# One more item in a layer's first group of matmuls, its split weights held in another pool

## The chip, the cores and the metric

The kernel runs on one NeuronCore of a Trainium2 chip. The metric is device time in microseconds (us) of one execution, the median over runs. The time before is 2758.85 us, the median of 3 runs (2755.78 to 2760.88).

## What is computed

The reference is one inference step of a two-layer trunk on 128 context tokens and 512 latent tokens (640 together), model width 1024. Each layer runs three mixers on one normalised input and then a feed-forward block. Cut to what the change touches:

```python
h = rms_norm(x, lp['g_pre1']) * (1 + sc1) + sh1
(cb, cc, cx, aq, ak, av, dn_q, dn_k, dn_v, dn_z, dn_beta, dn_a, gate_logits) = jnp.split(
    h @ lp['w_in'], SPLIT_IDX, axis=-1)
ya = (cb * depthwise_conv(cc * cx, lp['conv_w'])) @ lp['w_pa']
...
# gated DeltaNet, 4 heads of 128
qkv = jax.nn.silu(depthwise_conv(jnp.concatenate([q_raw, k_raw, v_raw], axis=-1), conv_w))
g = -jnp.exp(a_log) * jax.nn.softplus(a_logit + dt_bias)
...
o = rms_norm(o, norm_g) * jax.nn.silu(z)
```

The change is about `z = dn_z`, a 1024 by 512 slice of the input projection, 128 columns for each head. Its value is needed only at the end, when the head's output `o` is gated.

## The kernel before

**A linear layer.** Activations lie as 8 tiles of 128 channels by 640 tokens, each split into a high and a low part (`hh`, `hl`). A weight block is 128 x 4 x 128: it is loaded into `wraw` (L361 or L376, 256 KB, three buffers, issued by SyncE's queue SP), ScalarE (ACT) casts it to `whi` (L94), VectorE (DVE) forms `wlo` (L95), and TensorE (PE) runs three matmuls for each of 4 channel tiles (L365 to L367) on 320 tokens, which is half of them. So one output of 128 columns takes two blocks, and 24 matmuls for each half of the tokens. `whi` and `wlo` have four buffers each (`NW = 4`); a PSUM tile `l` has three (`NL = 3`), so the fourth `l` in a row waits until the first has been copied out.

**The group.** A layer begins with `group(items)`: it loads and splits the weights of all items, runs the first half of the tokens through all of them and then the second half, so the first half can run while the second half of `hh`, `hl` is still being made. Items with a pool name (`"C"`, `"E"`) hold their split weights there through both halves (`wkh`, `wkl`, or `wk` in `"E"`). The items are k, q, v of DeltaNet head 0, the gate logits (`lin`, L825, raw weights), and z of head 0. In layer 1 the previous layer's residual norm runs as `side`, one step after each item.

**What follows.** `gz()` is `dn_gates_tail`: matmuls `bgG` (L836, L850, L860) with a chain of small ACT and DVE steps in between (`bn`, `gb`), ending in `rws` (L862), which is written to memory (`gd`, L863) and read back four times, spread over partitions, as `rowb` (L917, three buffers). From `rowb` come `egl` (L972), `Dt` (L967, L977) and the rest of the DeltaNet preparation. Meanwhile `dn_post` runs k, q and v through a convolution (`dy`, L579 to L581, DVE), a sigmoid (`ds`, ACT) and a product (`dz`, DVE); `nat` (L911) transposes `dz` of k and v, and `kk` (L958) multiplies. The other linear layers are woven between these as filler (`fillc`), by costs that the generators yield: first z of the second head (`dn_z(l, 1)`), then the convolution branch (`cc`, whose first output is copied by L449 into `ccs`), while k, q, v of head 1 follow as `padc` (L873 copies). The Tile framework keeps each engine's instructions in the order in which it scheduled them, so on every engine an instruction that waits holds back all behind it.

Of the kernel before, what the change touches and what calls it, by code (L numbers as in the profile page):

```python
# [52 lines left out]
def tile_trunk(ctx: ExitStack, tc: tile.TileContext, I: dict, O: list, layers=DEPTH):  # L53
# [7 lines left out]
    def slot(name, shape=(P, NT), dt=F32, tag="F"):  # L61
        n = {"H": NH_, "C": NC_, "F": NF_}[tag]
        return sb.tile(list(shape), dt, tag=tag, name=name, bufs=n)
# [33 lines left out]
    def drain(g):  # L97
        for _ in g or ():
            pass
# [296 lines left out]
    def linear(src, acts, ev):  # L396


        pb = {}
        i0 = 0  # L400
        for hi, lo, nk in wblocks(src, len(acts)):
            for h in range(2):
                if i0 == 0:
                    pb[h] = lbank()[:, :HF]
                for j in range(nk):
                    ah, al = acts[i0 + j]
                    mm3(pb[h], hi[:, j, :], lo[:, j, :], hv(ah, h), hv(al, h), i0 + j == 0, i0 + j == len(acts) - 1)
                if i0 + nk == len(acts):
                    ev(h, pb[h])
            i0 += nk  # L410

    def group(items, side=None):


        bl = [b if callable(b) or isinstance(b, list) else wblocks(b, len(a), k) for b, a, _, k in items]
        for h in range(2):
            for b, (_, a, ev, _) in zip(bl, items):
                if callable(b):
                    b(h)
                else:  # L420
                    lin_half(b, a, h, ev)
                if h == 0:
                    next(side or iter(()), None)
            drain(side)

    def sig_ev(dst, keep=None, halves=False):

        def ev(h, pb):
            A.activation(hv(dst, h), pb, AF.Exp, scale=-1.0)  # L429
            if keep is not None:  # L430
                V.tensor_copy(hv(keep, h), pb)
            if halves:
                sig_tail(hv(dst, h))
            elif h:
                sig_tail(dst)
        return ev
# [24 lines left out]
    def store_x(src):  # L461
        for k in range(KD):
            SY.dma_start(out=xd[k], in_=src[k])
# [341 lines left out]
    def dn_gates(l):  # L805

        raw = slot("wg", (P, KD, 32), tag="C")
        G.memset(raw, 0.0)
        c0 = COL["beta"]
        SY.dma_start(out=raw[:, :, 0:16], in_=I["w_in"][l, :, c0:c0 + 16].rearrange("(k p) f -> p k f", p=P))  # L810
        dtal = small("dtal", (P, 2, 8), 2)
        SY.dma_start(out=dtal[:, 0], in_=I["dn_dt_bias"][l].rearrange("a b -> (a b)").partition_broadcast(P))
        SY.dma_start(out=dtal[:, 1], in_=I["dn_a_log"][l].rearrange("a b -> (a b)").partition_broadcast(P))
        A.activation(dtal[:, 1], dtal[:, 1], AF.Exp)
        hh = cur["h"]
        lg = slot("lg")

        def lin(h):

            pb = lbank()[:, :HF]  # L820
            for i in range(2):
                for a in range(2):
                    for j in range(4):
                        k = 2 * j + i
                        T.matmul(pb[32 * j:32 * j + 32], lhsT=raw[:, k, :], rhs=hv(hh[k][a], h).bitcast(F32),  # L825
                                 start=(i + a == 0), stop=(i + a == 2))
            A.copy(hv(lg, h), pb)

        return (lin, None, None, None), lambda: dn_gates_tail(l, lg, dtal)
# [36 lines left out]
    def dn_qkv(l, which, h):  # L866

        c0 = COL[("dq", "dk", "dv")[which]] + h * P
        t = padded("padc")

        def ev(h_, pb):
            for a, b, o in PS[h_]:
                A.copy(t[:, o:o + b - a], pb[:, a:b])  # L873

        return (I["w_in"][l, :, c0:c0 + P], cur["h"], ev, None), t
# [256 lines left out]
    def z_item(l, h):  # L1132
        c0 = COL["dz"] + h * P
        s, z = slot(f"zs{h}"), slot("zz")
        return (I["w_in"][l, :, c0:c0 + P], cur["h"], sig_ev(s, z)), s, z

    def dn_z(l, h, zs, first=None):
        item, s, z = first or z_item(l, h)
        if first is None:
            linear(*item)  # L1140
        V.tensor_mul(s, s, z)
        zs[h] = s
        yield 6.5
# [63 lines left out]
    def chain(*gens):  # L1207
        for g in gens:
            yield from g
# [52 lines left out]
    def lead(l):  # L1262

        qkv = [(w, dn_qkv(l, w, 0)) for w in (1, 0, 2)]
        item, gz = dn_gates(l)
        z0 = z_item(l, 0)

        items = [x[1][0][:3] + ("C",) for x in qkv] + [item, z0[0] + ("E",)]
        return gz, [(w, (None, x[1])) for w, x in qkv], z0, items

    cur["h"] = hh
    for p in range(2):
        mod_first(p)
        if p == 0:
            first = lead(0)
            for i in range(NLD):
                w, a, ev, k = first[3][i]
# [6 lines left out]
    for l in range(layers):  # L1284
        cur["h"] = hh
        on, zs, ya, yf, kv, o, mix, qs = {}, {}, [], [], [], [], [], {}
        gz, qkv, z0, items = first or lead(l)
        first = None
        group(items, side)
        gz = gz()  # L1290
        store_x(xs)

        def mainc():
            for hp in range(2):
                yield from delta_pair(l, hp, gz, on, qkv if hp == 0 else None)
                for h in (2 * hp, 2 * hp + 1):
                    yf.append(dn_out(l, h, on[h], zs[h]))
                    yield Y_DO
            yield from attn_kv(l, kv)
            yield from attn_q(l, 0, kv, qs)  # L1300
            pend = []
            for h in range(NH):
                stages, of = attn_head(l, h, kv, qs)
                for n, (fa, fb, pr2) in enumerate(stages):
                    args = () if pr2 is None else (pr2,)
                    sm_ = fa(*args)
                    yield Y_AT
                    pend.append((fb, args, sm_))
                    if len(pend) > NPD:
                        f_, a_, s_ = pend.pop(0)  # L1310
                        f_(*a_, s_)
                        yield Y_AT
                    if n == 0 and h + 1 < NH:
                        yield from attn_q(l, h + 1, kv, qs)
                o.append(of)
            for f_, a_, s_ in pend:
                f_(*a_, s_)

        def fillc():
            yield from dn_z(l, 0, zs, z0)  # L1320
            yield from dn_z(l, 1, zs)
            yield from conv_branch(l, ya)
            for h in (2, 3):
                yield from dn_z(l, h, zs)
            yield from branch(l, 0, ya, "w_pa", True)
            yield from gates(l, 2)
            yield from gates(l, 1, 0, NGB)
            while len(yf) < 4:
                yield None
            yield from weave(branch(l, 2, resplit(yf, "F"), "w_pc"), mods, PB)  # L1330


        mods = chain(mod_part(0, 2, 2), mod_part(0, 3, 2), mod_part(0, 4)) if l == 0 else iter(())
        drain(run(mainc(), fillc()))
        oo = resplit(o, "C")
        drain(weave(branch(l, 1, oo, "w_pb", res=mix, tag="C"), mods, PB))
        ys = [cslot(f"y{k}") for k in range(KD)]
        h2 = hslots("h2", "H")
        side = lin_res(I["w_o"][l], mix, ys, gsc[l][1], KEEP, False,
                       lambda h: prenorm_half(ys, h, gsc[l][2], modT[l][:, 24:32, :], h2), f32_of(h2), side=mods)  # L1340
        mods = iter(())
        if l + 1 < layers:
            drain(load_rows(l + 1))
            make_cols(l + 1)
            mods = chain(mod_part(l, 5), *[mod_part(l + 1, i) for i in range(6)])
        acts, acts2 = [], []
        g = ffn(l, h2, 0, F1, acts, LEAD, side)
        next(g)
        store_x(ys)
        drain(weave(g, mods, PF))  # L1350
        part = [cslot(f"pt{m}") for m in range(KD)]
        drain(weave(chain(fill_down(l, acts, part), ffn(l, h2, F1, KF, acts2)), mods, PF))
        drain(mods)
        if l + 1 < layers:
            hh = hslots("h", "H")
            after = lambda h: prenorm_half(part, h, gsc[l + 1][0], modT[l + 1][:, 0:8, :], hh)
            xe = f32_of(hh)
        else:
            after = lambda h: out_half(part, h)
            xe = [slot("xe", tag="H") for _ in range(KD)]  # L1360
        side = lin_res(I["w_down"][l, F1 * P:], acts2, part, gsc[l][3], KEEP, True, after, xe, l + 1 == layers)
        xs = part
# [63 lines left out]
```

## Time and profile before

| | |
|---|---|
| median of 3 runs | 2758.85 us (2755.78 to 2760.88) |
| profiled execution, its own time | 2755.11 us |
| its span in the trace | 2753.0 us |
| mean granted TensorE clock | 0.994 of full speed |
| PE busy | 2692.1 us, 98% of the span |
| DVE busy | 1564.1 us, 57% |
| ACT busy | 1256.7 us, 46% |
| mean DMA rate | 105 GB/s |

A busy share says how long an engine had an instruction in work, and an idle PE is time in which the next matmul of its fixed order was not ready. The times below are counted from the start of the span; layer 0's group lies at about 50 to 86 us, layer 1's at about 1414 to 1460 us.

### The profile page before, as it was taken

The page shows a single profiled execution, that of the slowest core. Times are in us where ns is not written, and L with a number is a line of the kernel's source. Part 1 is how long each engine was busy: PE and PEld are TensorE (multiplying, and loading weights), DVE is VectorE, ACT ScalarE, POOL GpSimd, SP SyncE. Part 2 cuts the span into 40 slices and gives each one's busy share as a digit, 9 for nine tenths or more (in the row PEclk, how much of TensorE's full clock was granted, in tenths as well). Part 3 has the DMA queues.
Part 4 walks back from the last instruction along what each step waited for, and adds up shares of the span by engine and source line. Part 5 has one row for each costly group of instructions (what it writes and reads, how often), then busy time and mean ns, then how long its engine had stood idle before and what let it go on. Part 6 is the DMA issues. An engine that isn't in the chain of part 4 may idle for free.

```text
span 2753.0 us, 49627 instructions
## 1 busy us (share of the span) xinstructions
PE 2692.1 (98%) x19706; PEld 2576.6 (94%) x19706; DVE 1564.1 (57%) x3385; ACT 1256.7 (46%) x2863; POOL 26.8 (1%) x148
## 2 busy tenths in 40 slices
PE   7999999999999999999999999999999999999998
PEld 3899998999899999999989999999999999999997
DVE  5586575477744744224476875754777465432344
ACT  4533554565534633223455345545655364332343
POOL 0000000000000000000000000000000000000001
PEclk9999999999999999999999999999999999999999
DMA  8542355533464344444533323333223532222241
GB/s 243 79 78 55 79 93 105 93 66 97 156 164 153 128 131 153 129 155 146 169 90 71 75 49 85 95 85 87 71 93 120 135 105 72 78 73 73 77 124 56
DMA packets 387800, 288.15 MB, mean 105 GB/s; under 512 B 18699, under 2 KB 348145, under 8 KB 387569
## 3 DMA queue, kind: packets, MB, share of 16 engines
q1 hardware_dynamic: 387568, 285.00, 39.5%
q8 instruction: 154, 2.52, 0.4%
q14 instruction: 78, 0.63, 0.1%
HBM read 251.86 MB, written 33.07 MB: 103 GB/s over the span
## 4 chain that ended last, share of the span: by engine, by line
PE 84%; DVE 7%; DMA 4%; ACT 3%; issue 1%; SPq 0%; POOL 0%; DVEq 0%; ACTq 0%
PE l L365 23%; PE l L366 23%; PE l L367 23%; PE pm L326 1%; DMA wraw<-in_w_in_dram 1%; DMA wm<-in_w_mod_dram 1%; PE ptT L785 1%; DMA rowb<-gd 1%; PE po L795 1%; PE scan L1083 1%; PE po L797 1%; PE sco L365 1%; PE po L796 1%; DVE Tt L1002 1%; PE scan L1091 1%
## 5 line engine op out<-in xcount | busy, mean ns | idle before, releaser
L94 ACT CAST whi<-wraw 128x512 fp32r<-128x512 f32 (+1 forms) x540 | 332.3, 615 | 840.6 <-PE l L366 796.1
L95 DVE TENSOR_TENSOR wlo<-wraw,whi 128x512 fp32r<-128x512 f32 (+1 forms) x540 | 367.1, 681 | 525.7 <-ACT whi L94 512.6
L365 PE MATMUL l<-hh,whi 128*128 128x320 f32 x1856 | 587.0, 316 | 3.1 <-ACT ccs L449 3.1
L366 PE MATMUL l<-hl,whi 128*128 128x320 f32 x1856 | 579.8, 312 | 0.0
L367 PE MATMUL l<-hh,wlo 128*128 128x320 f32 x1856 | 579.3, 312 | 0.0
L365 PE MATMUL l<-h2h,whi 128*128 128x320 f32 x1248 | 387.4, 310 | 0.0
L366 PE MATMUL l<-h2l,whi 128*128 128x320 f32 x1248 | 385.3, 309 | 0.0
L367 PE MATMUL l<-h2h,wlo 128*128 128x320 f32 x1248 | 385.3, 309 | 0.0
L365 PEld LDWEIGHTS l<-hh,whi 128*128 128x128 f32 x1856 | 349.8, 188 | 6.8 <-ACT ccs L449 3.6
L366 PEld LDWEIGHTS l<-hl,whi 128*128 128x128 f32 x1856 | 349.9, 189 | 1.9
L367 PEld LDWEIGHTS l<-hh,wlo 128*128 128x128 f32 x1856 | 349.7, 188 | 1.0
L365 PEld LDWEIGHTS l<-h2h,whi 128*128 128x128 f32 x1248 | 234.6, 188 | 7.0 <-ACT fs L429 3.1
L366 PEld LDWEIGHTS l<-h2l,whi 128*128 128x128 f32 x1248 | 234.7, 188 | 0.0
L367 PEld LDWEIGHTS l<-h2h,wlo 128*128 128x128 f32 x1248 | 234.6, 188 | 0.0
L365 PE MATMUL l<-ah,whi 128*128 128x320 f32 x544 | 169.0, 311 | 0.0
L366 PE MATMUL l<-al,whi 128*128 128x320 f32 x544 | 168.2, 309 | 0.0
L367 PE MATMUL l<-ah,wlo 128*128 128x320 f32 x544 | 168.0, 309 | 0.0
L365 PE MATMUL l<-rsh,whi 128*128 128x320 f32 x384 | 119.7, 315 | 0.0
L366 PE MATMUL l<-rsl,whi 128*128 128x320 f32 x384 | 118.4, 312 | 0.0
L367 PE MATMUL l<-rsh,wlo 128*128 128x320 f32 x384 | 118.2, 309 | 0.0
L365 PEld LDWEIGHTS l<-ah,whi 128*128 128x128 f32 x544 | 102.2, 188 | 2.2 <-issue 1.3
L367 PEld LDWEIGHTS l<-ah,wlo 128*128 128x128 f32 x544 | 102.3, 188 | 0.0
(428 smaller groups left out, 5299.2 us busy)
## 6 DMA issues: line engine op xcount, KB each, us to landing
wraw<-in_w_in_dram SPq DMA_DIRECT2D x256, 256.0 KB, 4.9
wm<-in_w_mod_dram SPq DMA_DIRECT2D x80, 512.0 KB, 4.7
wraw<-in_w_gate_dram SPq DMA_DIRECT2D x88, 256.0 KB, 2.9
wraw<-in_w_up_dram SPq DMA_DIRECT2D x88, 256.0 KB, 3.3
wraw<-in_w_down_dram SPq DMA_DIRECT2D x80, 256.0 KB, 2.9
mixo<-mixd SPq DMA_DIRECT2D x32, 320.0 KB, 5.9
wm<-in_w_mod_dram SPq DMA_DIRECT2D x32, 256.0 KB, 4.7
wraw<-in_w_pb_dram SPq DMA_DIRECT2D x32, 256.0 KB, 2.8
```

The lines of the kernel that those rows point to most:

```text
L94: A.copy(hi, src)
L95: V.tensor_sub(lo, src, hi.bitcast(F32))
L326: T.matmul(pm[32 * u:32 * u + 2, 0:256], lhsT=sc[:, k, :], rhs=w[:, u * 256:(u + 1) * 256], start=(n == 0), stop=(n == KD - 1))
L365: T.matmul(out, lhsT=wh, rhs=ah, start=first, stop=False)
L366: T.matmul(out, lhsT=wh, rhs=al, start=False, stop=False)
L367: T.matmul(out, lhsT=wl, rhs=ah, start=False, stop=last)
L785: T.transpose(pt[:, i, q * P:(q + 1) * P], sm_[q][:, kt * P:(kt + 1) * P], ident)
L795: T.matmul(po, lhsT=vh, rhs=th, start=(kt == 0), stop=False)
L796: T.matmul(po, lhsT=vl, rhs=th, start=False, stop=False)
L797: T.matmul(po, lhsT=vh, rhs=tl, start=False, stop=(kt == 4))
L1002: V.tensor_add(Tt[:, j + 1:32, 0:j], Tt[:, j + 1:32, 0:j], tv)
L1083: T.matmul(pst[:, 1, :], lhsT=XT[h, d][:, c, :], rhs=r, start=True, stop=True)
```

## The change

`lead(l)` adds a sixth item to the group: z of head 1, with its two blocks of split weights held in pool `"F"`. `fillc`'s `dn_z(l, 1)` gets that item handed in and no longer issues loads, splits and matmuls for it. It still yields its cost to the weaver.

```diff
         z0 = z_item(l, 0)
 
-        items = [x[1][0][:3] + ("C",) for x in qkv] + [item, z0[0] + ("E",)]
-        return gz, [(w, (None, x[1])) for w, x in qkv], z0, items
+        z1 = z_item(l, 1)
+        items = [x[1][0][:3] + ("C",) for x in qkv] + [item, z0[0] + ("E",), z1[0] + ("F",)]
+        return gz, [(w, (None, x[1])) for w, x in qkv], (z0, z1), items
...
         def fillc():
-            yield from dn_z(l, 0, zs, z0)
-            yield from dn_z(l, 1, zs)
+            for h in range(2):
+                yield from dn_z(l, h, zs, z0[h])
             yield from conv_branch(l, ya)
```

The number of matmuls, loads and splits is the same. Three places where rows move:

On ACT in layer 0, behind the first half of the group, the order before is this (`whi_937`, `whi_943` are z of head 1, `whi_1094`, `whi_1100` the first `cc` output, `padc_368` is k of head 0, `padc_372` q):

```order
91 L94 CAST whi_943<-wraw_941 128x512
92 L429 ACTIVATE zs0_388<-l_681 128x320
93 L94 CAST whi_1094<-wraw_1092 128x512
94 L94 CAST whi_1100<-wraw_1098 128x512
95 L873 COPY padc_368<-l_708 128x320
96 L882 ACTIVATE ds_877<-dy_873 128x641
```

And this is the same place in the changed kernel:

```order
92 L429 ACTIVATE zs0_388<-l_695 128x320
93 L94 CAST whi_1094<-wraw_1092 128x512
94 L94 CAST whi_1100<-wraw_1098 128x512
95 L94 CAST whi_1170<-wraw_1168 128x512
96 L429 ACTIVATE zs1_390<-l_722 128x320
97 L94 CAST whi_1176<-wraw_1174 128x512
98 L873 COPY padc_368<-l_749 128x320
99 L882 ACTIVATE ds_947<-dy_943 128x641
```

The casts of two more blocks, 1170 and 1176 (k of head 1), now stand ahead of the copy of k and of its convolution; before, they stood behind `ds` of v, since z of head 1 held two of the four buffers. DVE's `wlo` of the two blocks moves the same way, ahead of `dy` of k.

On PE in layer 0 the rows behind the group before are these, from the last of the 48 matmuls of z of head 1 that stand there (`whi` from row 290) on:

```order
286 L365 MATMUL l<-hh_316,whi 128x320
287 L366 MATMUL l<-hl_317,whi 128x320
288 L367 MATMUL l<-hh_316,wlo 128x320
289 L850 MATMUL bgG<-bn,cst 128x40 x2
290 L365 MATMUL l<-hh_318,whi 128x320
```

In the changed kernel this is what follows the group (`whi` is here the first `cc` output):

```order
311 L836 MATMUL bgG<-cst,lg 128x16 x5
312 L911 MATMUL nat<-ident,dz 128x128 x6
313 L365 MATMUL l<-hh_310,whi 128x320
314 L366 MATMUL l<-hl_311,whi 128x320
315 L367 MATMUL l<-hh_310,wlo 128x320
316 L911 MATMUL nat<-ident,dz 128x128 x4
317 L958 MATMUL kk<-dz 128x128 x3
...
324 L958 MATMUL kk<-dz 128x128 x2
325 L850 MATMUL bgG<-bn,cst 128x40 x2
326 L958 MATMUL kk<-dz 128x128 x2
327 L860 MATMUL bgG<-ident,gb 40x128
```

The 48 matmuls are gone from here. Five of the six `nat` rows are k's, the sixth is the first of v, and it stands ahead of almost all the filler. 24 matmuls of z of head 1 stand at the end of each half of the group instead.

On ACT in layer 1, at the norm of the second half of the tokens (`pn`, `rs`, `hh0`), the order before is this (`whi_16411`, `whi_16417` are the first `cc` output):

```order
1366 L94 CAST whi_16411<-wraw_16409 128x512
1367 L94 CAST whi_16417<-wraw_16415 128x512
1368 L130 ACTIVATE rs_15796<-pn_15794,eps_68 128x320
1369 L131 ACTIVATE rs_15796<-rs_15796 128x320
1370 L188 ACTIVATE hh0_15041<-hv_15894,modT1_296 128x320
```

In the changed kernel:

```order
1370 L130 ACTIVATE rs_15796<-pn_15794,eps_68 128x320
1371 L94 CAST whi_16487<-wraw_16485 128x512
1372 L131 ACTIVATE rs_15796<-rs_15796 128x320
1373 L429 ACTIVATE zs1_15821<-l_16027 128x320
1374 L188 ACTIVATE hh0_15041<-hv_15908,modT1_296 128x320
1375 L94 CAST whi_16493<-wraw_16491 128x512
1376 L188 ACTIVATE hh1_15043<-hv_15939,modT1_296 128x320
```

Here too the casts of the next two blocks (k of head 1) have come forward, into the norm that makes the second half's `hh`.

## Rows read from the trace of the kernel before

**Rows 1.** The page's first part: busy time, share and instructions.
```profile
PE 2692.1 (98%) x19706; PEld 2576.6 (94%) x19706; DVE 1564.1 (57%) x3385; ACT 1256.7 (46%) x2863; POOL 26.8 (1%) x148
```

**Rows 2.** PE's waits from 50 to 118 us: releaser, total us, times, longest.
```profile
PE l L365 <- ACT ccs L449: 2.7, 1, 2.7
PE bgG L850 <- DVE bn L846: 2.4, 1, 2.4
PE bgG L836 <- ACT lg L827: 1.0, 1, 1.0
```

**Rows 3.** PE's timeline, layers 0 and 1: start, us, work, [idle before].
```profile
85.92 0.51 PE L836 MATMUL bgG<-cst,lg 128*128 128x16 f32 x4
...
99.46 2.39 PE L958 MATMUL kk<-dz 128*128 128x128 f32 x20
...
102.73 0.40 PE L365 MATMUL l<-hh,whi 128*128 128x320 f32 x1
...
114.53 0.64 PE L365 MATMUL l<-hh,whi 128*128 128x320 f32 x1 [2.75 <-ACT ccs L449]
...
1436.93 0.81 PE L157 MATMUL pn<-acc,ones 128*128 128x320 f32 x2 [1.45 <-DVE acc L152]
...
1442.24 1.17 PE L365 MATMUL l<-hh,wkh 128*128 128x320 f32 x3 [4.15 <-ACT hh L188]
...
1482.67 0.42 PE L365 MATMUL l<-hh,whi 128*128 128x320 f32 x1 [0.33 <-ACT ccs L449]
```

**Rows 4.** Three stretches: length, each engine's busy us, PEclk, DMA share, GB/s.
```profile
76.00:84.00 8.00, 8.00 (x71) 6.45 (x70) 4.59 (x8) 3.79 (x8) 0.00 (x0) 1.00 1.02 67
...
114.00:117.50 3.50, 2.97 (x11) 2.98 (x12) 2.36 (x4) 1.94 (x5) 0.00 (x0) 0.51 0.28 76
...
1438.40:1445.20 6.80, 2.96 (x11) 2.93 (x12) 5.04 (x11) 3.81 (x8) 0.00 (x0) 0.50 0.52 102
```

**Rows 5.** SP's loads in layer 0, and the page's median to landing.
```profile
67.11 11.41 SPq L361 DMA_DIRECT2D wraw<-in_w_in_dram  x6
...
wraw<-in_w_gate_dram SPq DMA_DIRECT2D x88, 256.0 KB, 2.9
```

**Rows 6.** ACT's timeline in layer 0, from the last casts to `padc` of head 1.
```profile
76.78 0.62 ACT L94 CAST whi<-wraw 128x512 fp32r<-128x512 f32 x1 [0.67 <-DMA wraw<-in_w_in_dram]
77.30 0.42 ACT L873 COPY padc<-l 128x320 f32<-128x320 f32 x1
...
90.73 0.20 ACT L839 ACTIVATE bn<-bgG 128x40 f32<-128x40 f32 x1
...
96.29 0.26 ACT L862 COPY rws<-bgG 40x128 f32<-40x128 f32 x1
...
113.95 0.21 ACT L972 ACTIVATE egl<-rowb 128x5 f32<-128x5 f32 x1 [4.94 <-DMA rowb<-gd]
...
114.37 0.74 ACT L977 ACTIVATE Dt<-Dt 128x640 f32<-128x640 f32 x1
...
119.65 0.49 ACT L873 COPY padc<-l 128x128 f32<-128x128 f32 x2 [1.29 <-PE l L367]
```

**Rows 7.** DVE's timeline in layer 0: `dy` of k and `dz` of v.
```profile
78.04 0.55 DVE L579 TENSOR_SCALAR dy<-padc,cols 128x641 f32<-128x641 f32 x1
...
94.83 0.29 DVE L885 TENSOR_TENSOR dz<-dy,ds 128x128 f32<-128x128 f32 x1 [0.21 <-ACT ds L440]
```

**Rows 8.** ACT's and DVE's timelines in layer 1: the norm, the gates, `padc`.
```profile
1439.46 0.62 ACT L94 CAST whi<-wraw 128x512 fp32r<-128x512 f32 x1 [1.60 <-DMA wraw<-in_w_in_dram]
1439.98 0.52 ACT L130 ACTIVATE rs<-pn,eps 128x320 f32<-128x320 f32 x1
...
1461.68 0.20 ACT L839 ACTIVATE bn<-bgG 128x40 f32<-128x40 f32 x1
...
1467.59 0.24 ACT L862 COPY rws<-bgG 40x128 f32<-40x128 f32 x1
...
1487.26 0.48 ACT L873 COPY padc<-l 128x128 f32<-128x128 f32 x2
...
1441.04 1.48 DVE L187 SCALAR_TENSOR_TENSOR hv<-pt,gsc,rs 128x320 f32<-128x320 f32 x3 [0.24 <-ACT rs L131]
```

## Prediction, made before the changed kernel ran

> **What bounds the kernel now.** I read the page's busy shares first. PE works for 2692.1 of 2753.0 us [rows 1], so 61 us of idle is all that any reordering could win, and the change adds or removes no work on any engine: the same matmuls, loads and splits stand elsewhere. I then read PE's waits and its timeline around the two groups, to see whose results it lacks there. In layer 0 the longest waits from 50 to 118 us are 2.7 us for the copy `ccs`, 2.4 us for `bn` of the gates chain and 1.0 us for `lg` [rows 2]. In layer 1 two waits of 1.45 and 4.15 us stand at the norm of the second half [rows 3]. So both groups are places where z of head 1 can serve as filler, and the question is what else its move changes.
>
> **Price of the work moved.** From 102.73 to 111.78 (114.53 less the idle of 2.75 before it) PE ran 60 matmuls of a linear layer [rows 3], 0.15 us each. The 24 of a half take 3.6 us, the 48 of z of head 1 take 7.2 us. They cost nothing extra; they only win what idle they fill and lose what they used to fill.
>
> **Layer 0, the splits that come forward.** Before, z of head 1 held two of the four `whi`/`wlo` buffers; now these go to the next two blocks, 1170 and 1176 (k of head 1), and their casts stand on ACT ahead of the copy `padc` of k, their `wlo` on DVE ahead of `dy` of k. Before, that copy came at 77.30, right behind the cast of 76.78 [rows 6], and `dy` of k at 78.04 [rows 7], 1.26 us after the cast began. Now it comes 1.26 us after the cast of block 1176 can begin. When does that block land? SP issues six blocks between 67.11 and 78.52 [rows 5]; the last but one is 1176's, and it waits for a raw buffer that is freed by the split of the first `cc` block, at about 76.8. From 76 to 84 us the DMA engines are busy all the time and move only 67 GB/s [rows 4]: 262 kB take 3.9 us. Block 1170's load goes first, from 76.8 to 80.7, then 1176's until 84.6, and `dy` of k begins at 85.9, 7.8 us late. The other end is a landing 2.9 us after the issue, the page's median for blocks of another matrix [rows 5]: 79.7, `dy` of k at 81.0, 3.0 us late. The measured rate of that very stretch is the nearer row, but I can't see each block's landing; I take 7 us late.
>
> The Trainium skill (DMA: Bandwidth & Descriptors, Anatomy of one DMA) gives, for transfers issued from GpSimd, about 2.0 us and then the bytes at 436 GB/s; 262 kB would take an estimated 2.6 us by that page, and the sum for layer 0 would be about that of the early end. Here the 2.9 us agree with it and the 67 GB/s don't.
>
> **Layer 0, the chain behind it.** k, q and v go through DVE and ACT one after the other, from `dy` of k at 78.04 to `dz` of v at 94.83 [rows 7], 16.8 us in which each step waits for the one before. I move it by 7: `dz` of v begins at 101.8 and is done about 1 us later. PE leaves the group earlier. It left at 85.92 [rows 3]; 7.2 us of z come on top, and about 3 us more of waiting inside the group: z's blocks of head 1 land no sooner than before, and the second half of k, which used to run while PE waited for a split, now stands behind them. So PE is at the first transpose of v at about 97 and waits until 102.8, some 5.5 us, in place of the 1.0 and 2.4 us of before. It then has left to do what PE before had done by 102.73: `kk` and `dqr` (99.46 to 102.73 [rows 3], 3.3 us) and some 1.4 us of small transposes and `bgG`. Its lag is then about 4.8 us.
>
> The gates chain is later still. Its first ACT step (L839) ran at 90.73, ahead of `ds` of v; now it stands behind it, so it starts at about 102, and `rws`, 5.56 us behind it [rows 6], at 107.8, 11.5 us late. The extra ACT copies of `nat` and `kk` now between them are covered by the steps of z's sigmoid that left. From `rws` the four `rowb` reads follow on SP with the same three buffers, so the last lands 11.5 us late too: `egl` at 125.5 for 113.95 [rows 6]. Behind that `egl` ACT has `Dt` (ended 1.16 us after `egl` began [rows 6]) and then the copies `padc` of head 1's k (0.49 us): done at 127.1. Before, that copy waited only for PE (119.65 [rows 6]).
>
> What waits for it: with three PSUM tiles `l`, the third linear half behind the one that began at 114.53 needs the tile which this `padc` copies out. That is 48 matmuls behind 114.53. Eleven ran at half clock until 117.5 (granted 0.51 [rows 4]), 37 more at 0.15 us: it began at 123.0 before. PE's own lag of 4.8 us, less the 2.75 us for `ccs` (whose copies now stand ahead of the late `egl`) and less the 1.3 us that the half clock cost there, would bring it there at about 123.7. So PE waits for `padc`, until 127.1: 4.1 us later than before. The clock fell to 0.5 after the idle of 2.75 us and of 4.15 us [rows 3, 4]; if it falls again behind such a wait, eleven matmuls at half clock lose 1.3 us. I count 0.9. **Layer 0: +5.0 us.** With `dy` of k only 3.0 us late the copy is done at 123.1 and the term is +0.1; with 7.8 us, and the whole loss by the clock, it is +6.2.
>
> **Layer 1.** The first half of z of head 1 (3.6 us) now stands ahead of and around `pn`, in the 5.6 us of idle [rows 3]. But the cast of block 16487 stands between the two ACT steps of the norm, and its `wlo` ahead of `hv` on DVE. Before, the cast ended just ahead of L130 at 1439.98 and `hv` followed at 1441.04 [rows 8]. A cast (0.62 [rows 8]) and a `wlo` about as long, partly side by side, make `hv` about 1.2 us later, between 0.5 and 2; PE resumes at 1443.4 for 1442.24, with 3.6 us more done, a gain of 2.4 us. Behind the group the gates chain pays: 3.6 us of z now stand ahead of its first `bgG`, so L839 comes up to 4.8 us later than 1461.68. The rest of the chain used to be held on PE by z's matmuls in between (`rws` at 1467.59, 5.91 us behind [rows 8]) and no longer is, and half of the stretch at half clock (1438.4 to 1445.2 [rows 4]) may go: I take 3 us late for `rws`, between 2 and 4.8. `padc` (done at 1487.74 [rows 8]) then is done at 1490.7. PE needed it 48 matmuls behind 1482.67 [rows 3], at 1489.8 or so, so it had 2 us in hand. Now it comes there 2.4 us sooner and waits until 1490.7. **Layer 1: +0.9 us**; I take +0.7, since part of the 3 us is uncertain. The ends are -2.4 (the chain not late) and +2.7.
>
> **The sum.** +5.0 and +0.7 are +5.7 us. Against the profiled execution's 2755.11 us (span 2753.0) that is 2760.8 us; the median of the runs lies 3.74 us above that execution, so I predict 2764.5 us for a median of 2758.85, slower by 0.2%, which is just about what a measurement of this kernel tells from no change (5.5 us). The shift stays to the end, because from there on PE is busy nearly all the time.
>
> **Rivals.**
> 1. *The two blocks land early* (2.9 us as in rows 5, not 3.9 us each one after the other). Then layer 0 ends at +0.1 and layer 1 at +0.7: 2759.7 us, no change. For it speaks that less else may be in flight once the order on SP has changed, and the page of the skill named above; against it the full DMA share at 67 GB/s in that stretch [rows 4].
> 2. *Faster: the gates chain isn't late.* If `rws` in both layers comes early enough that no `padc` holds PE (less than 6 us late in layer 0, less than 0 in layer 1), only the filling counts: the wait of 2.75 us for `ccs` and the half clock behind it go (4 us) and layer 1 gains 2.4 us, 6.4 us in all: 2752.5 us. It would need `dy` of k less than about 2 us late, which is sooner than the fast load gives, so little speaks for it.
> 3. *Slower by more.* If the waits of layer 0 come one behind another, at the transposes, at `bgG` L850 and L860 (now with little filler ahead of them) and at `padc`, each with half clock behind it, and L839 of layer 1 comes the whole 4.8 us late: +6.2, +1.3 for a second drop, +2.7, together some 10 us: 2769 us.
> 4. *Only a move.* The same work in the same waits: 2758.85 us. Against it stands the order itself, in which `dy` of k waits for two more loads.
>
> **Chances.** The forecast 0.60 (of it two thirds above the 5.5 us, one third within), rival 1 0.17, rival 2 0.10, rival 3 0.08, rival 4 0.05. So faster 0.10, same 0.42 (0.20, 0.17 and 0.05), slower 0.48. The range goes from 2755, which leaves out rival 2, to 2771, which takes in rival 3; the likeliest case's own range, by its bounds, is 2760 to 2768.
>
> **What would show it.** In the changed kernel: the cast of block 1176 between 82 and 85 us and `dy` of k right behind it; an idle PE of some 5 us ahead of a `nat` at 97 to 103 us; `rws` at 107 to 109; no wait for the first `ccs`; a PE wait for `padc` ending at about 127. In layer 1 the idle ahead of `hh` down from 5.6 to some 3 us, and a new wait of 2 to 3 us for `padc` at about 1490. It is wrong if block 1176 lands by 80 us, if DVE takes `dy` of k without delay, or if PE finds other work in the 5 us.

## The result, and the profile after

The changed kernel takes 2772.28 us (median of 6 runs, 2769.26 to 2778.01) against 2757.98 us for the kernel before in the same comparison: a ratio of 1.0052, interval 1.0041 to 1.0063, some 14 us slower. The prediction had slower, but 2764.5 us, and the measured time lies just beyond its range of 2755 to 2771.

Where the time lies shows best in two stretches that hold the same work in both kernels: each begins where PE, at the start of a layer's group, stops waiting for `hh`, and ends where it begins the triangular solve of the first heads (`pw`, L1030). These are the rows of the stretches of the kernel before (columns: stretch, length, busy us and instructions of PE, weight loads, DVE, ACT and POOL, granted clock, DMA share, GB/s):

```profile
58.43:204.88 146.45, 138.18 (x974) 133.41 (x974) 108.08 (x241) 68.21 (x171) 3.42 (x26) 0.99 0.54 85
1415.48:1571.90 156.42, 148.22 (x1023) 142.00 (x1024) 123.81 (x283) 79.57 (x197) 3.42 (x26) 0.97 0.37 88
```

And of the kernel after:

```profile
59.59:213.51 153.92, 139.06 (x975) 133.26 (x975) 107.78 (x241) 68.57 (x171) 3.44 (x26) 0.99 0.50 81
1427.15:1590.56 163.41, 152.11 (x1023) 145.61 (x1024) 123.30 (x283) 79.62 (x197) 3.45 (x26) 0.94 0.36 84
```

Layer 0 is 7.5 us longer, layer 1 7.0 us, together 14.5. The profiled execution of the changed kernel (2775.84 us, span 2772.1) lies 3.6 us above its median; its span is 19.1 us above that of before, and of the 4.6 us that are not in the two stretches 1.2 lie at the start and 3.0 between the two, where the last section shows a drop of the clock. Times of layer 1 below are compared with 11.67 us taken off (1427.15 less 1415.48), those of layer 0 with 1.16 us off.

PE's timeline of the kernel after, in layer 0 and layer 1 (start, us, work, idle before and who ended it), against [rows 3]:

```profile
106.05 0.47 PE L911 MATMUL nat<-ident,dz 128*128 128x128 f32 x1 [3.97 <-DVE dz L885]
...
130.32 0.41 PE L365 MATMUL l<-hh,whi 128*128 128x320 f32 x1 [2.48 <-ACT padc L873]
...
1454.32 0.90 PE L365 MATMUL l<-hh,wkh 128*128 128x320 f32 x2 [2.64 <-ACT hh L188]
...
1505.88 0.64 PE L365 MATMUL l<-hh,whi 128*128 128x320 f32 x1 [6.39 <-ACT padc L873]
```

The waits are those that were forecast: at the first transpose of v, at `padc` of head 1 in both layers, and a shorter one for `hh` in layer 1 (2.64 us for 1.45 and 4.15). The 2.75 us for `ccs` is gone. The one that is far larger than forecast is the wait for `padc` in layer 1, 6.39 us.

ACT's timeline of the kernel after, layer 0 first and then layer 1, against [rows 6, 8]:

```profile
79.44 0.62 ACT L94 CAST whi<-wraw 128x512 fp32r<-128x512 f32 x1 [0.87 <-DMA wraw<-in_w_in_dram]
...
83.90 0.62 ACT L94 CAST whi<-wraw 128x512 fp32r<-128x512 f32 x1 [3.84 <-DMA wraw<-in_w_in_dram]
...
87.52 0.62 ACT L94 CAST whi<-wraw 128x512 fp32r<-128x512 f32 x1 [2.66 <-DMA wraw<-in_w_in_dram]
88.05 0.42 ACT L873 COPY padc<-l 128x320 f32<-128x320 f32 x1
...
105.89 0.20 ACT L839 ACTIVATE bn<-bgG 128x40 f32<-128x40 f32 x1
...
112.05 0.24 ACT L862 COPY rws<-bgG 40x128 f32<-40x128 f32 x1
...
129.06 0.21 ACT L972 ACTIVATE egl<-rowb 128x5 f32<-128x5 f32 x1 [4.05 <-DMA rowb<-gd]
...
129.80 0.80 ACT L873 COPY padc<-l 128x128 f32<-128x128 f32 x3
...
1478.55 0.19 ACT L839 ACTIVATE bn<-bgG 128x40 f32<-128x40 f32 x1
...
1483.57 0.25 ACT L862 COPY rws<-bgG 40x128 f32<-40x128 f32 x1
...
1495.26 0.21 ACT L972 ACTIVATE egl<-rowb 128x5 f32<-128x5 f32 x1 [4.05 <-DMA rowb<-gd]
...
1504.10 0.21 ACT L972 ACTIVATE egl<-rowb 128x5 f32<-128x5 f32 x1 [5.43 <-DMA rowb<-gd]
...
1505.35 0.81 ACT L873 COPY padc<-l 128x128 f32<-128x128 f32 x3
```

The casts are those of the second `cc` block (79.44), of 1170 (83.90) and of 1176 (87.52). The last stands right ahead of `padc` of k, as forecast. The rest of the chain in layer 0 is late by 14.0 us at `bn`, 14.6 us at `rws` and 14.0 us at the last `egl`. In layer 1 it is late by 5.2 us at `bn`, 4.3 us at `rws`, and then by 7.6 us at the last `egl` (1504.10 less 11.67 against 1484.83 before). The first and the last `egl` of layer 1 on ACT's timeline of the kernel before:

```profile
1476.71 0.21 ACT L972 ACTIVATE egl<-rowb 128x5 f32<-128x5 f32 x1 [0.20 <-DMA rowb<-gd]
...
1484.83 0.21 ACT L972 ACTIVATE egl<-rowb 128x5 f32<-128x5 f32 x1 [1.36 <-DMA rowb<-gd]
```

DVE's timeline of the kernel after in layer 0, against [rows 7]:

```profile
88.78 0.55 DVE L579 TENSOR_SCALAR dy<-padc,cols 128x641 f32<-128x641 f32 x1
...
105.70 0.29 DVE L885 TENSOR_TENSOR dz<-dy,ds 128x128 f32<-128x128 f32 x1 [0.57 <-ACT ds L440]
```

`dy` of k is 9.6 us late, `dz` of v 9.7: between the two nothing is won back, as forecast.

SP's issues of the kernel after, the loads of layer 0, that of block 1176 among them by itself, and the reads of layer 1:

```profile
69.92 19.34 SPq L361 DMA_DIRECT2D wraw<-in_w_in_dram  x8
...
79.32 0.37 SPq L361 DMA_DIRECT2D wraw<-in_w_in_dram  x1
...
1483.85 0.31 SPq L863 DMA_DIRECT2D gd<-rws  x1
1486.03 0.37 SPq L361 DMA_DIRECT2D wraw<-in_w_in_dram  x1
1486.45 11.14 SPq L917 DMA_DIRECT2D rowb<-gd  x4
```

The loads behind the group begin at 69.92 for 67.11 before [rows 5], 1.7 us late with the 1.16 us off. In layer 1 a weight load now stands between `gd` and the `rowb` reads. In the kernel before it stood behind the first two:

```profile
1470.43 0.94 SPq L917 DMA_DIRECT2D rowb<-gd  x2
1471.46 0.48 SPq L361 DMA_DIRECT2D wraw<-in_w_in_dram  x1
1471.99 6.78 SPq L917 DMA_DIRECT2D rowb<-gd  x2
```

### The profile page after: what moved, and what is told of

Read it like the earlier page. It is cut to its first block, busy times and chain, and to the rows that moved or that the text cites. A ratio compares the mean times of both kernels' runs of the same rounds, so it can differ in the third digit from the quotient of the medians.

```text
span 2772.1 us, 49618 instructions
## 1 busy us (share of the span) xinstructions
PE 2701.0 (97%) x19706; PEld 2582.5 (93%) x19706; DVE 1564.4 (56%) x3385; ACT 1257.6 (45%) x2863; POOL 26.9 (1%) x148
## 4 chain that ended last, share of the span: by engine, by line
PE 84%; DVE 6%; DMA 5%; ACT 3%; issue 1%; SPq 0%; POOL 0%; DVEq 0%; ACTq 0%
PE l L365 23%; PE l L366 23%; PE l L367 23%; DMA wraw<-in_w_in_dram 2%; PE pm L326 1%; DMA rowb<-gd 1%; DMA wm<-in_w_mod_dram 1%; PE ptT L785 1%; PE po L795 1%; PE scan L1083 1%; PE po L797 1%; PE sco L365 1%; PE po L796 1%; PE kk L958 1%; PE scan L1091 1%
## 5 line engine op out<-in xcount | busy, mean ns | idle before, releaser
L365 PE MATMUL l<-hh,whi 128*128 128x320 f32 x1824 | 579.0, 317 | 9.7 <-ACT padc L873 9.5
L366 PE MATMUL l<-hl,whi 128*128 128x320 f32 x1824 | 571.8, 314 | 0.0
L367 PE MATMUL l<-hh,wlo 128*128 128x320 f32 x1824 | 571.4, 313 | 0.0
```

Source lines behind the costliest of these rows:

```text
L365: T.matmul(out, lhsT=wh, rhs=ah, start=first, stop=False)
L366: T.matmul(out, lhsT=wh, rhs=al, start=False, stop=False)
L367: T.matmul(out, lhsT=wl, rhs=ah, start=False, stop=last)
```

## The experiments

Theory A: the casts that pool F lets forward hold up k's copy and convolution. Theory B: the cost is the second half of z of head 1 in the group, behind which the gates chain starts later and has less to cover it. All runs are compared with the kernel before; the last two columns are the stretches defined above, of one profiled execution each, 146.45 and 156.42 us before.

| kernel | median us | ratio (interval) | layer 0 us | layer 1 us |
|---|---|---|---|---|
| the change | 2772.28 | 1.0052 (1.0041 to 1.0063) | 153.92 | 163.41 |
| e1_none: weights not in F | 2764.98 | 1.0026 (1.0015 to 1.0036) | 149.16 | 160.20 |
| e7_half_F: second half behind the group | 2765.93 | 1.0022 (1.0013 to 1.0032) | 150.09 | 155.68 |
| e5_half: both of these | 2755.30 | 0.9987 (0.9979 to 0.9996) | 143.48 | 155.77 |
| e2_l0: change in layer 0 only | 2767.44 | 1.0031 (1.0019 to 1.0043) | 154.94 | 157.48 |
| e3_l1: change in layer 1 only | 2765.82 | 1.0025 (1.0016 to 1.0035) | 147.13 | 162.88 |
| e4_keepF: only the pool | 2762.76 | 1.0010 (1.0002 to 1.0019) | 150.30 | 154.37 |
| e9_before_nl4: before, 4 `l` tiles | 2771.76 | 1.0048 (1.0033 to 1.0063) | 145.80 | 155.81 |
| e8_after_nl4: the change, 4 `l` tiles | 2792.99 | 1.0124 (1.0111 to 1.0137) | 158.67 | 161.72 |
| e12_before_early: before, gates early | 2766.79 | 1.0027 (1.0017 to 1.0038) | 146.42 | 167.27 |
| e10_after_early: the change, gates early | 2772.33 | 1.0045 (1.0032 to 1.0057) | 151.92 | 166.68 |
| e11_half_early: e5_half, gates early | 2761.50 | 1.0008 (0.9999 to 1.0017) | 144.94 | 162.36 |
| e13_load: before, one more read | 2767.52 | 1.0027 (1.0016 to 1.0038) | 144.85 | 163.88 |

The kernel of before stood at 2759.16 us beside the first four experiments, at 2760.30 beside the next four and at 2759.49 beside the last four.

**The pool and the second half, each undone (e1_none, e7_half_F, e5_half).** The first edit takes pool F away:

```diff
-... + [item, z0[0] + ("E",), z1[0] + ("F",)]
+... + [item, z0[0] + ("E",), z1[0] + (None,)]
```

The other two run the first half of z of head 1 in the group and the second behind `gz()`, in pool F (e7_half_F) or in the `whi`/`wlo` buffers (e5_half):

```diff
+        late = [(wblocks(b, len(a), k), a, ev) for b, a, ev, k in late]
         for h in range(2):
...
+            if h == 0:
+                for b, a, ev in late:
+                    lin_half(b, a, 0, ev)
...
             yield from dn_z(l, 0, zs, z0[0])
+            for bb, a, ev in late:
+                lin_half(bb, a, 1, ev)
+            yield from dn_z(l, 1, zs, z0[1])
```

> All of the change stays but one word: z of head 1 takes its split weights from the four whi/wlo buffers again instead of pool F, so the casts of blocks 1170 and 1176 (and 16487, 16493 in layer 1) can't come forward. Theory A (the casts that come forward hold up k's copy and convolution in layer 0 and the norm in layer 1): dy of k in layer 0 begins near 79 to 80 us instead of 88.8, the PE wait of 3.97 us at the first transpose of v is gone, and the kernel is within 5 us of before. Theory B (it is the 48 matmuls taken from behind the group, and the gates chain that starts later for it): rws is still 6 us or more late in layer 0 and 4 us late in layer 1, and the time stays 8 us or more above before.

> As the run with the first half in the group and the second behind it, but with the split weights in pool F, so that the casts of the next two blocks come forward as in the change. Theory A: dy of k in layer 0 again at 87 to 89 us, hv in layer 1 about a microsecond late, and 7 us or more slower than before. Theory B: within 4 us of before, because the gates chain has its filler back.

> Only the first half of z of head 1 runs in the group; its second half (24 matmuls) stands behind the start of the gates chain, where all 48 stood before, and its split weights come from the whi/wlo buffers. Theory A: near the run with whi/wlo buffers and both halves in the group, since the early casts are gone in both. Theory B: the first ACT step of the gates chain is ahead of ds of v again, rws is at most 2 to 3 us late, PE waits for no padc, and the idle of 5.6 us ahead of hh in layer 1 is filled by 3.5 us, so the kernel comes out 2 to 4 us faster than before, and some 5 us or more ahead of the run with both halves in the group.

With the kernel after these are the four corners of a square, and both theories hold part of it. In layer 0 pool F costs 6.6 us (150.09 less 143.48) or 4.8 (153.92 less 149.16), and the second half in the group 5.7 or 3.8. In layer 1 pool F costs -0.1 or 3.2 us, and the second half 4.4 or 7.7. So in layer 0 both cost, by amounts that single profiles don't tell apart, and B is the larger part in layer 1. The runs say the same of the two layers together: by ratio pool F costs 9.7 or 7.2 us and the second half 10.8 or 8.3. They differ from the sums of the profiles by up to 3 us, and no finer than that is the split by layers. Two of the expectations fell: e1_none, by ratio 7 us slower, was neither within 5 us nor 8 us or more above, and e7_half_F was neither 7 us slower nor within 4, but 6. DVE's first row of k's convolution shows A's part, first in e1_none, with the wait at the transpose gone:

```profile
80.94 0.56 DVE L579 TENSOR_SCALAR dy<-padc,cols 128x641 f32<-128x641 f32 x1
```

and then in e7_half_F, where it is back behind the cast of 1176 (88.60, after ACT had waited 2.67 us for its load):

```profile
89.86 0.55 DVE L585 TENSOR_SCALAR dy<-padc,cols 128x641 f32<-128x641 f32 x1
```

B's part is PE's wait for `padc` of head 1. In e1_none, without the early casts, it stands in both layers, and in layer 1 it is the longest of its kind in any run:

```profile
122.98 0.63 PE L365 MATMUL l<-hh,whi 128*128 128x320 f32 x1 [4.06 <-ACT padc L873]
...
1500.51 0.64 PE L365 MATMUL l<-hh,whi 128*128 128x320 f32 x1 [7.30 <-ACT padc L873]
```

In e5_half PE's waits of layer 1 for `hh` and for `padc` are both below 3 us:

```profile
1445.69 0.56 PE L365 MATMUL l<-hh,wkh 128*128 128x320 f32 x2 [2.49 <-ACT hh L188]
...
1491.39 0.41 PE L365 MATMUL l<-hh,whi 128*128 128x320 f32 x1 [2.86 <-ACT padc L879]
```

e5_half is the version that beats both kernels, by 3.6 us (0.9987) against before: it keeps the first half of z in the group and gives the second back to the gates chain. The number was as expected, the place was not. The expectation had the gain in layer 1, in the idle ahead of `hh`; by the profile 3.0 us of it lie in layer 0, where the waits for `lg`, `bn` and `ccs` [rows 2] are gone, and only 0.65 in layer 1, where the wait for `padc` is new.

**One layer at a time (e2_l0, e3_l1).** The sixth item for one `l` only:

```diff
-        z1 = z_item(l, 1)
+        z1 = z_item(l, 1) if l == 0 else None
...
+        if l == 0:
+            items.append(z1[0] + ("F",))
...
```

> The change in layer 0 only; layer 1 as before. Leaves layer 0's part: the two profiles give 7.5 us (from the wait for hh of the second half to the first RB wait: 146.45 us before, 153.92 after). Both theories: 6 to 9 us slower than before. If it is 12 us or more, layer 1's part was not its own but carried over.

> The change in layer 1 only; layer 0 as before. If the two layers' costs simply add, this leaves what the run with layer 0 alone did not show: 14.3 less 8.3 us, so 5 to 8 us slower than before, with a PE wait of 5 to 7 us for padc behind the gates. If layer 1's cost was carried over from a late layer 0, it is within 3 us of before. The prediction's own term for layer 1 was 0.7 us.

Both came as expected: 8.6 us by ratio for layer 0, 6.9 us for layer 1, 15.5 together for the 14.3 of the change. So layer 1's cost is its own, not carried over from layer 0, and 0.7 us was wrong for it. PE's wait in e3_l1:

```profile
1501.66 0.63 PE L365 MATMUL l<-hh,whi 128*128 128x320 f32 x1 [6.38 <-ACT padc L873]
```

**Only the pool (e4_keepF).** z of head 1 stays behind the group:

```diff
-            linear(*item)
+            linear(*item, keep="F" if h == 1 else None)
```

> The matmuls of z of head 1 stay behind the group as before; only its split weights go to pool F, so that two of the four whi/wlo buffers are free for the next blocks. If the freed buffers cost by themselves (some 9 to 10 us between the two pairs of runs that differ only in the pool): 6 to 11 us slower than before. If they cost only because the casts that come forward land ahead of k's copy, which the scheduler needn't do here: the casts of 1170 and 1176 stand behind that copy and among the steps of ds of k, so dz of k comes 2 to 5 us later than before, and the 7 us of matmuls behind the group hide most of it: 0 to 4 us slower.

2.8 us by ratio: the freed buffers cost little where the scheduler puts the casts behind k's copy and the 48 matmuls stay behind the group. The casts still hold up k's sigmoid: `dz` of k comes 6 us later than before, more than the 2 to 5 us expected. PE's waits for `lg` and `bn` in layer 0 grew to 3.4 and 3.2 us (1.0 and 2.4 in [rows 2]).

```profile
91.10 0.90 PE L836 MATMUL bgG<-cst,lg 128*128 128x16 f32 x6 [3.43 <-ACT lg L827]
...
100.95 0.61 PE L850 MATMUL bgG<-bn,cst 128*128 128x40 f32 x4 [3.18 <-DVE bn L846]
```

**Is it the PSUM tile? (e8_after_nl4, e9_before_nl4).**

```diff
-NL, NB = 3, 5
+NL, NB = 4, 4
```

> The change, with four PSUM tiles l and four c instead of three and five. If PE's late waits (2.5 us in layer 0 and 6.4 us in layer 1, each for the padc copy of head 1) are waits for a free l tile, they go or shrink below 1.5 us, and it stands only 4 to 9 us above the kernel of before with the same tiles. If the wait is for data of the late chain, it stays: 12 us or more above that kernel.

> The kernel of before with four PSUM tiles l and four c: the control for the run above. The wait of 2.75 us for ccs in layer 0 is one for an l tile and goes; the c tiles are fewer for the DeltaNet and attention steps, which may cost: between 4 us faster and 10 us slower than before.

The waits for `padc` shrink to below 0.5 us in layer 0 and 0.85 us in layer 1, so they are waits for a free `l` tile. But the gap between the two kernels is 21 us, not 4 to 9: PE now waits for `dz` of head 1 instead (5.16 and 3.76 us), so the tile is only where the late chain is felt. The fewer `c` tiles cost by themselves (e9_before_nl4 is 13 us slower than before by ratio, where at most 10 were expected), and no run shows that they cost the same in both kernels, so the 21 us are not split further. PE's timeline of e8_after_nl4:

```profile
163.02 0.47 PE L911 MATMUL nat<-ident,dz 128*128 128x128 f32 x1 [5.16 <-DVE dz L885]
...
1519.60 0.41 PE L365 MATMUL l<-hh,whi 128*128 128x320 f32 x1 [0.85 <-ACT padc L873]
...
1544.27 0.47 PE L911 MATMUL nat<-ident,dz 128*128 128x128 f32 x1 [3.76 <-DVE dz L885]
```

**The gates chain early (e10_after_early, e11_half_early, e12_before_early).** The second half takes the gate logits second, and the tail is issued behind q:

```diff
+            order = range(len(items)) if h == 0 or gz is None else [0, 3, 1, 2] + list(range(4, len(items)))
+            for i in order:
+                b, (_, a, ev, _) = bl[i], items[i]
...
+                if h and gz and i == 1:
+                    tail = gz()
```

> The change, but in the second half of the group the gate logits run second, right behind k, and the tail of the gates chain is issued behind q instead of behind the whole group. If the late gates chain is what holds PE at padc (2.5 us in layer 0, 6.4 us in layer 1), rws comes some 8 to 15 us earlier in both layers, these two waits go below 1 us, and the kernel is 6 to 11 us faster than the change as it stands (2761 to 2766 us). If the convolution chain behind the early casts holds PE by itself, the waits for dz of v stay and grow, and it gains less than 4 us.

> The run with z's first half in the group and the second behind it, weights in whi/wlo, which measured 2755.3 us, with the gate logits second in the second half as well. If the remaining wait for padc in layer 1 (2.86 us) is the gates chain's, it goes: 2 to 5 us faster, 2750 to 2753 us. If rowb's arrival on ACT ahead of ds of v holds up the convolutions instead: slower by up to 5 us.

> The kernel of before with the gate logits second in the second half: the control for the two runs above. PE's waits for bn (2.35 us) and ccs (2.75 us) in layer 0 belong to the same chain; they go, and z of head 1 then fills nothing: 2 to 6 us faster than before. If the early chain disturbs k, q and v: within 2 us of before or slower.

In none of the three did the gain come that was hoped for; what came is the other case that each expectation names, in e11_half_early with 6 us where up to 5 were expected. The late gates chain can't be cured so: before becomes 7 us slower, the change stays within 2 us of itself by ratio, e5_half loses its gain. The waits for `padc` do go in layer 0 and shrink to 1.39 us in layer 1, but in layer 1 the `egl` steps now stand on ACT ahead of `ds` of v and wait there for `rowb`, so `dz` of v is late and PE waits for that. ACT's timeline of e10_after_early in layer 1:

```profile
1482.19 0.21 ACT L977 ACTIVATE egl<-rowb 128x5 f32<-128x5 f32 x1 [4.02 <-DMA rowb<-gd]
...
1485.36 0.72 ACT L887 ACTIVATE ds<-dy 128x641 f32<-128x641 f32 x1
```

and PE's:

```profile
1488.00 0.47 PE L916 MATMUL nat<-ident,dz 128*128 128x128 f32 x1 [4.49 <-DVE dz L890]
...
1514.36 0.41 PE L365 MATMUL l<-hh,whi 128*128 128x320 f32 x1 [1.39 <-ACT padc L878]
```

These runs therefore don't say how much of the change's cost is the gates chain's alone.

**Bytes ahead of the reads (e13_load).**

```diff
+            if l == 1 and h == 0:
+                SY.dma_start(out=spare, in_=gd[l][:, 7, :].partition_broadcast(P))
             Gbs = [rowb(l, 4 * d + h) for d in range(2)]
```

> The kernel of before with one more read of 320 KB from gd (to spare memory) on SP ahead of the four rowb reads of layer 1. In all runs with both halves of z in layer 1's group, 11.5 to 11.8 us pass there from rws to the first egl, in the others 8 to 10. If that is bytes in flight ahead of rowb, it goes from 9.1 to 11 to 13 us here; the time moves by 0 to 3 us, as PE has 2 us in hand. If it is not, it stays below 10 us.

From `rws` to the first `egl` 12.65 us pass, for 9.1 before: a transfer ahead of the reads can lengthen them. Of the 3.5 us, 1.2 pass before the first read is issued and 2.3 behind that. The time was off: 7.5 us by ratio where 0 to 3 were expected, all of it in layer 1's stretch. PE's wait for `ccs`, which stands behind that `egl` on ACT, grew from 0.33 [rows 3] to 4.86 us. That 0.33 had said already that nothing was in hand there; the 2 us that I had worked out are those of `padc`. ACT's timeline of e13_load:

```profile
1470.32 0.24 ACT L862 COPY rws<-bgG 40x128 f32<-40x128 f32 x1
...
1482.97 0.21 ACT L975 ACTIVATE egl<-rowb 128x5 f32<-128x5 f32 x1 [3.73 <-DMA rowb<-gd]
```

and PE's:

```profile
1489.93 0.64 PE L365 MATMUL l<-hh,whi 128*128 128x320 f32 x1 [4.86 <-ACT ccs L449]
```

## Why the prediction was wrong in size

**Layer 0, right in mechanism, +5.0 predicted, +7.5 measured.** Every step was there: the cast of 1176 ahead of `padc` of k, the 16.9 us from `dy` of k to `dz` of v (16.8 before), the wait at the first transpose, `rws` late, `padc` as the last wait. The term mis-sized is the first: `dy` of k was 9.6 us late, not 7 and not within the bound of 7.8. The rate was right: the casts of the second `cc` block, of 1170 and of 1176 (79.44, 83.90 and 87.52) lie 4.5 and 3.6 us apart, for 3.9 forecast. What I had wrong is that I let the loads begin when they did before. The first of them waits for a raw buffer, which a split in the group frees; that split came later too, and the load began 1.7 us later. Block 1176's own, which takes the raw buffer of the first `cc` block, was issued 1.3 us later (79.32 less 1.16 for 76.85). I had also let the load of 1170 begin at 76.8, though in the kernel before it was issued at 74.02. The early end, 2.9 us to landing, was a row of another matrix; the trace of before has a row for the blocks of this one, issued between 50 and 100 us, and it says 5.5:

```profile
wraw<-in_w_in_dram SPq DMA_DIRECT2D x11, 256.0 KB, 5.5
```

The delay then grows from 9.7 us at `dz` to 14.6 us at `rws`, 4.9 us more, where I had added 4.5. At the last `egl` it was 14.0 us, for 11.5 forecast. The wait at the transpose (3.97 us for 5.5) was shorter, because PE came there later itself: inside the group it had waited 1.9 us for a copy `padc` at 68, 2.8 us for splits and casts, and 1.4 us for `padc` at 93. Behind `padc` of head 1 PE resumed 6.2 us later than before (130.32 less 1.16 for 122.97), where I had added 4.1; two shorter waits behind it (0.67 and 0.36 us, for 0.14 before) make 0.9, and the last 0.4 of the 7.5 I don't split. The half clock that I had counted at 0.9 us behind `padc` didn't come in this profile; the clock stood at half from 105.4 to 108.8 instead, behind the wait at the transpose, where PE had 2.48 us of waiting still to come.

**Layer 1, +0.7 predicted, +7.0 measured: the step that failed.** The gain was there: the wait for `hh` went from 5.6 us in two parts to 2.64 us in one, and PE resumed only 0.4 us later than before, with half of z more behind it. `rws` was 4.3 us late, between the 3 that I took and the bound of 4.8. What failed is the step "`padc` then is done at 1490.7", which carried `rws`'s delay on unchanged. From `rws` to the last `egl` 20.5 us pass instead of 17.2, 3.3 us more, and 2.6 of them lie ahead of the first `egl`, which comes 11.7 us behind `rws` instead of 9.1. What changed there on SP is that a weight load of 256 KB which stood behind the first two `rowb` reads now stands ahead of them. e13_load shows that a transfer there can do this (12.65 us). It is not the only way: in e1_none no load stands between `gd` and `rowb`, but two stand just ahead of `gd`, the first read is issued 4.6 us behind `rws` for 2.8, and 11.7 us pass there too. In e3_l1 and e8_after_nl4 the same order comes with 11.8 and 11.5 us in layer 1. But the order is not enough: in layer 0 of e9_before_nl4 a load stands in the same place, 0.4 us ahead of the first read, and the first `egl` comes only 9.1 us behind `rws` (100.75). SP's issues and ACT's step there:

```profile
102.85 0.37 SPq L361 DMA_DIRECT2D wraw<-in_w_in_dram  x1
103.27 2.37 SPq L917 DMA_DIRECT2D rowb<-gd  x3
...
109.85 0.21 ACT L972 ACTIVATE egl<-rowb 128x5 f32<-128x5 f32 x1 [1.23 <-DMA rowb<-gd]
```

So the longer round trip is measured, and the order on SP is a likely cause of it, not one that is shown; what else it needs stays open. PE waits for the second of the three `padc` copies, which was done at 1494.2 (1505.83 less 11.67), 6.4 us later than before and 3.4 later than forecast: 1.3 from `rws` and 3.3 from the reads, less 1.2 that the steps between the last `egl` and the copies took less. PE waited 6.39 us. Behind this wait the clock stood at half (0.50) for 21 matmuls, where I had counted nothing; this is the stretch in the kernel after:

```profile
1506.30:1511.40 5.10, 5.10 (x21) 5.10 (x21) 5.03 (x11) 0.62 (x1) 0.00 (x0) 0.50 0.42 121
```

At 0.15 us each those 21 would take 3.1 us, so 2.0 are lost. With the 4.4 us that PE resumed late (1494.2 for 1489.8) that is 6.4 of the 7.0; the rest I don't split.

**Rivals.** The third came nearest (some 10 us for the 14.3). Its waits at the transposes and at `padc` came, L839 of layer 1 was 5.2 us late, beyond its whole 4.8, and the clock fell behind a wait in each layer; its waits at `bgG` didn't come, and it had nothing for the reads. The first and the fourth fell with the cast at 87.5 us; the second can't have been, as `padc` held PE in both layers. e5_half comes nearest to what the second rival would have needed, filling without a late chain, and it gains 3.6 of that rival's 6.4 us.

Block 1176 was cast at 86.4 us (87.52 less 1.16), 1.8 us later than the landing that I had worked out from the rate of 67 GB/s, and 8.2 us behind its issue at 79.32, with ACT idle for it in the last 2.66. The Trainium skill (DMA: Bandwidth & Descriptors, Anatomy of one DMA) gives about 2.0 us and then the bytes at 436 GB/s for transfers issued from GpSimd, an estimated 2.6 us for a block; the trace does not agree with that for these loads, which SP issues, several of them in flight.

## What to carry to other kernels

When work is moved, look not only at the engine that does it but at what its buffers let forward: two loads that had nothing to do with z were scheduled ahead of the critical copy because two buffers were free. Filler has a place where it covers a chain of small steps; take half of it if half fills the earlier idle, and leave the rest. And carry a delay through a DMA only with the queue's new order in hand: behind a load or a read that had moved ahead of it, a small round trip became 2.6 us longer in the changed kernel and 3.5 us in e13_load, though not in e9_before_nl4.

## What the hardware showed that was not expected

The clock also fell where PE had not waited at all. In the profiled execution of the changed kernel PE was busy without a gap from 455 us on, with a good part of its instructions matmuls of 32x32 and 64x64, and then the granted clock was 0.61 in one stretch and 0.50 in the next:

```profile
463.00:466.40 3.40, 3.40 (x25) 2.75 (x26) 1.64 (x4) 2.39 (x5) 0.00 (x0) 0.61 0.22 40
466.40:469.00 2.60, 2.60 (x11) 2.60 (x11) 2.31 (x5) 0.00 (x0) 0.00 (x0) 0.50 0.53 180
```

The same place ran at full clock in the profile before, and at half in five of the other profiles. Why it falls in one execution and not in another, no run here shows. From the end of layer 0's stretch to the `scan` (L1079) behind this place the two profiles have the same 2254 matmul records, and the changed kernel takes 3.3 us longer (267.0 for 263.7). So single executions differ by up to some 3 us here, and that is a reason to read a change of a few us from many runs and not from two profiles.
